# Attention's row sums divided out in the block turning, by a diagonal matrix, instead of on GpSimd

## The chip, the cores and the metric

The kernel runs on one core of a Trainium2 chip. The metric is device time in microseconds for one execution of the whole layer, from runs on the chip. The core's engines are TensorE (PE; its weight loads are listed apart as PEld), VectorE (DVE), ScalarE (ACT), GpSimd (POOL) and SyncE (SP), which here only issues DMAs.

## The reference

One decoder layer: a sequence of 1024 rows of width 1024, in float32. The part that matters is the forgetting attention, 8 heads of width 64:

```
s = einsum('bhqd,bhkd->bhqk', qi, kh) * scale
s = s + ci[..., None] - cum[:, :, None, :]
s = where(key_pos <= q_pos, s, -inf)
p = softmax(s, axis=-1)
out = einsum('bhqk,bhkd->bhqd', p, vh)
```

Beside it stand four retention heads of width 128, computed in chunks of 128 rows; both groups go through one output projection, a layer norm, a gated MLP with a short convolution, and a second layer norm.

## The kernel before, in words

The program is straight-line code. It runs through stages: the conditioning and the retention heads (to about 239 us of the profile), the projection of the attention's values, the attention (about 272 to 492 us), the output projection, the up-projection and the down-projection. Up to the attention, the order of the engines' work is set by hand (a helper that queues each instruction behind the last one) and by a planner; from the attention on, each engine issues its instructions in the order of the program text, except where a line pins one behind another (`tc.issue_after`).

Nearly all large matmuls work on pairs of a high and a low half in the F32R type, so that a product of two F32 values is three matmuls. A few small products of the retention (`pS`, `po`) use plain F32 operands on 128x128 tiles, and so do the transposes, which multiply by the identity `ident` in transpose form (`pq`, `py`, `nT` and the attention's `pt`).

The attention is one loop of 8 heads x 8 row tiles of 128 rows, here called steps, and four more steps to drain it. A step `s_` of head `h` and row tile `i` does this, in the order of the text:

1. a piece of the projection of queries and keys, of this head or the next (`fox_proj`, lines 765 to 767), 6 matmuls of 512 columns;
2. `fox_scores` (lines 796 to 812): the scores of the row tile against the keys up to the diagonal, in a two-bank PSUM tile `ps`; on DVE, the sum with the bias row and the row's minimum `mn` (the scores are negated) into the SBUF tile `S`, 128 x (i+1)*128; on ACT, the exponential of the negated tile, with the row sums `den`; on DVE, the reciprocal of `den`; on GpSimd (line 813), `S` times the reciprocal, in place;
3. at odd steps, `fox_pv` (line 851) of a pair of row tiles: values times probabilities;
4. `fox_turn` (lines 824 to 842) of the row tile of three steps ago (`LAG = 3`): each 128x128 block of `S` is transposed on TensorE into a PSUM bank `pt`, up to four blocks a bank; ACT copies the bank into the high half of the probabilities, and DVE subtracts to make the low half.

There are 36 blocks a head, 288 in all, in 96 banks. `pt` comes from a ring of four PSUM banks, shared with the projections `qk` and the products `pv`. `S` tiles come from rings of SBUF slots; `dn` and `mn` are small tiles of one column.

The only work of GpSimd in this stage is line 813. The retention's small tiles `sT` and `R` (tags `sT` and `Rs`, three buffers each, 128x128 in F32) have their last use before the attention begins.

Of the kernel before, what the change touches and what calls it, by code (L numbers as in the profile page):

```python
# [8 lines left out]
F32 = mybir.dt.float32  # L9
# [4 lines left out]
ALU = mybir.AluOpType  # L14

P = 128
S = 1024
D = 1024
NT = S // P
# [12 lines left out]
def kernel(  # L32
# [23 lines left out]
    nc = tc.nc  # L56
# [5 lines left out]
    sp = ctx.enter_context(tc.tile_pool(name="sp", bufs=1))  # L62
# [4 lines left out]
    def slot(tag, shape, dtype, name, padded=None):  # L67
        return gp.tile(shape, dtype, tag=tag, bufs=NB[tag], name=name, padded_shape=padded)
# [4 lines left out]
    def small(shape, name):  # L73
        return sp.tile(shape, F32, tag="s", bufs=24, name=name)

    def f(ap):
        return ap.bitcast(F32)


    ident = cp.tile([P, P], F32, tag="ident", name="ident")  # L80
# [10 lines left out]
        out=maskb, in_=maskb, pattern=[[-1, P]], compare_op=ALU.is_ge,  # L91
# [5 lines left out]
        out=tri, in_=tri, pattern=[[1, P]], compare_op=ALU.is_ge,  # L97
# [39 lines left out]
    def bank2(name):  # L137
        return ps.tile([P, 1024], F32, tag="A", bufs=2, name=name)

    def bank(name):  # L140
        return ps.tile([P, 512], F32, tag="B", bufs=4, name=name)
# [173 lines left out]
    for i in (0, 2):  # L315
        queued("DVE", nc.vector.tensor_scalar,
               out=bcol[:, i, :], in0=bcol[:, i, :], scalar1=1.0, scalar2=None, op0=ALU.add)
# [24 lines left out]
    for j in range(ND):  # L342
# [28 lines left out]
        for t in range(3):  # L371
            for c in range(7):
                in_turn(first[c], (hi, hi, lo)[t][:, c * P:(c + 1) * P],
                        w0[j][:, (0, 1, 0)[t], :],
                        start=(j == 0 and t == 0), stop=(j == ND - 1 and t == 2))
# [4 lines left out]
    def ret_proj(h, c, ws, part, pt):  # L380
        if part == 0:

            pt = bank(f"rp{h}_{c}") if (h, c) == (0, NT - 1) else bank2(f"rp{h}_{c}")[:, :512]
        for j in range(4 * part, 4 * part + 4):
            three(pt, hhi[j][:, c * P:(c + 1) * P], hlo[j][:, c * P:(c + 1) * P],
                  ws[j][:, 0, :], ws[j][:, 1, :], j == 0, j == ND - 1, in_turn)
        return pt
# [166 lines left out]
    for n in range(RH * NT):  # L554
        h, c = divmod(n, NT)
# [51 lines left out]
    for m in range(NT - 1, RH * NT):  # L607
        h, c = divmod(m, NT)
# [3 lines left out]
        pt = ret_proj(h, c, ws, 0, None)  # L612
# [137 lines left out]
    def fox_alloc(h):  # L750
        t = {n: slot("X", [P, S], F32R, f"{n}{h}") for n in ("qh", "ql", "ks")}
        t["nb"] = slot("X" if h < 2 else "VM", [P, S], F32, f"nb{h}")
        pins["nb"] = nc.sync.dma_start(t["nb"], bass.AP(
            tensor=cum_d.tensor, offset=cum_d.offset + h * S, ap=[[0, P], [1, S]]))
        return t
# [27 lines left out]
    def fox_scores(h, i, T, beside=None):  # L783
        qh, ql, ks, nb = T["qh"], T["ql"], T["ks"], T["nb"]
        span = (i + 1) * P
        tag = "S" if i % 2 == 0 else "R" if h < FH - 1 else "VM"
        Ssb = slot(tag, [P, S], F32, f"S{h}_{i}")
        cuts = [(0, min(max(span, 256), 512))]
        if span > 512:
            cuts.append((512, max(span, 768)))  # L790
        mn = small([P, 1], f"mn{h}_{i}")
        qs = slice(i * P, (i + 1) * P)
        pt = bank2(f"ps{h}_{i}")
        for k0, k1 in cuts:
            last = k0 <= i * P < k1
            nc.tensor.matmul(pt[:, k0:k1], qh[:, qs], ks[:, k0:k1], start=True, stop=False)
            nc.tensor.matmul(pt[:, k0:k1], ql[:, qs], ks[:, k0:k1],
                             start=False, stop=not last)
            if last:
                nc.tensor.matmul(pt[:, i * P:(i + 1) * P], identb, maskb,  # L800
                                 start=False, stop=True)
        pins["min"] = nc.vector.tensor_tensor_reduce(  # L802
            out=Ssb[:, :span], in0=pt[:, :span], in1=nb[:, :span], scale=1.0, scalar=3e38,
            op0=ALU.add, op1=ALU.min, accum_out=mn,
        )
        if beside is not None:
            beside()
        den = small([P, 1], f"dn{h}_{i}")
        pins["exp"] = nc.scalar.activation(  # L809
            Ssb[:, :span], Ssb[:, :span], AF.Exp, scale=-1.0, bias=mn, accum_out=den,  # L810
        )
        nc.vector.reciprocal(den, den)  # L812
        nc.gpsimd.tensor_tensor(  # L813
            out=Ssb[:, :span], in0=Ssb[:, :span], in1=den.to_broadcast([P, span]),
            op=ALU.mult,
        )
        return Ssb

    PT = {}

    def fox_turn(h, i, Ssb):
        g, qo = divmod(i, 2)
        nkb = 2 * g + 2
        if qo == 0:
            PT[h, g] = [[slot("X", [P, 4, 256], F32R, f"pt{h}_{g}_{t}_{u}") for u in range(2)]
                        for t in range((nkb + 3) // 4)]
            for u in range(2):
                nc.vector.memset(  # L828
                    f(PT[h, g][(nkb - 1) // 4][u][:, (nkb - 1) % 4, 0:128]), 0.0)
        for t in range((i + 4) // 4):  # L830
            kbs = range(4 * t, min(4 * t + 4, i + 1))
            n = len(kbs)
            pt = bank(f"pt{h}_{i}_{t}")
            for kb in kbs:
                nc.tensor.transpose(  # L835
                    pt[:, (kb % 4) * P:(kb % 4 + 1) * P], Ssb[:, kb * P:(kb + 1) * P], ident
                )
            src = pt[:, :n * P].rearrange("p (k q) -> p k q", q=P)
            dh = PT[h, g][t][0][:, :n, qo * P:(qo + 1) * P]
            dl = PT[h, g][t][1][:, :n, qo * P:(qo + 1) * P]  # L840
            nc.scalar.copy(dh, src)  # L841
            nc.vector.tensor_tensor(out=dl, in0=src, in1=f(dh), op=ALU.subtract)  # L842

    def fox_pv(h, g):
# [4 lines left out]
        for kb in range(nkb):  # L849
            for u in range(2):  # L850
# [12 lines left out]
                            op=ALU.mult)  # L863
# [124 lines left out]
    def park_high(k):  # L988
        hi, raw = park[k]
        nc.scalar.copy(hi.bitcast(F32R), raw)  # L990

    def park_low(k):

        if k in park:
            hi, raw = park[k]
            with tc.issue_after(pins["min"].ins):
                nc.vector.tensor_tensor(out=raw.bitcast(F32R), in0=raw, in1=hi, op=ALU.subtract)
# [125 lines left out]
    Sb = {}  # L1123

    def proj(h, i):
        if i < 3:
            fox_proj(h, w, T[h], 1, i + 1)
        elif h + 1 < FH:
            fox_proj(h + 1, w, T[h + 1], *divmod(i - 3, 4))

    for s_ in range(FH * NT + LAG + 1):
        h, i = divmod(s_, NT)
        if h < FH:
            if i == 0:
                if h % 4 == 0:
                    for half in range(2):
                        mixF[h // 4, half] = slot("VM", [P, 2, 512], F32, f"mixF{h // 4}_{half}")
            if i == 3:
                w = nw
                if h + 1 < FH:  # L1140
                    T[h + 1] = fox_alloc(h + 1)
            if i >= 3:
                proj(h, i)
            k = LOWS.get(s_)
            Sb[s_] = fox_scores(h, i, T[h], None if k is None else lambda: park_low(k))
            if i == 4 and h + 2 < FH:
                nw = fox_w(h + 2)
            if i == 6:
                down_base(h)
            if k is not None:  # L1150
                park_store(k)
            for v, k in LOWS.items():
                if s_ == max(v - 4, 0):
                    park_load(k)
                if s_ == v - 2:
                    with tc.issue_after(pins["exp"].ins):
                        park_high(k)
        r = s_ - LAG - 1
        if r >= 0 and r % 2 == 1:
            fox_pv(r // NT, (r % NT) // 2)  # L1160
        r = s_ - LAG
        if 0 <= r < FH * NT:
            fox_turn(r // NT, r % NT, Sb.pop(r))
        if h < FH and not (i >= 3):
            proj(h, i)
        if h == FH - 1 and i == 0:
            for q in range(2):
                op_load(q)
            g_row = slot("S", [P, D], F32, "g_row0")
            nc.sync.dma_start(g_row, bcast_rows(gates[0], D))  # L1170
        if h == FH - 1:
            for m in LOADS.get(i, ()):
                wo_load(m)
            if i in (2, 3):
                op_split(i - 2, 1)
            if i >= NT - 2:
                op_half(0, 1, i - NT + 2)
        if s_ == FH * NT:
            for q in range(2):
                x_load(q)  # L1180
                sos[q] = slot("X", [P, S], F32, f"so{q}")
        if s_ == FH * NT + 1:
            op_mm(1, 1)
            op_split(0, 0)
# [440 lines left out]
    for pi, p in enumerate(PORD[:-1]):  # L1625
# [4 lines left out]
        start, stop = p in (1, 2, 5), p in (2, 3)  # L1630
        for k in range(NK):
# [5 lines left out]
            else:  # L1637
                for i in range(4):
                    d_mm(p, k, i, pts[i], start and k == 0, stop and k == NK - 1)
                    if p == 7 and k == NK - 1:  # L1640
                        add = nc.vector.tensor_tensor(  # L1641
                            out=s5[i], in0=s5[i], in1=X_[i], op=ALU.add)
# [105 lines left out]
```

## Time and profile before

| | us |
|---|---|
| median of 3 runs | 1215.36 (1215.21 to 1215.37) |
| span of the profiled execution | 1214.8 |
| runs beyond the span | about 0.6 |
| TensorE busy in the span | 1198.3 |
| DVE busy | 910.9 |
| ACT busy | 653.9 |
| GpSimd busy | 229.0 |
| of that, line 813 | 73.5 |

The profile is of one execution; its span runs from the first to the last instruction, and the device time has a little more around it. Times are in microseconds unless marked ns. A line of a group gives the source line, the engine, the operation, out<-in by the program's names, the shapes, the count, and then either the minimum, median and maximum of its durations, or busy time, mean ns of one and the idle time before it with what ended that. Matmuls overlap in the array, so that their durations are longer than the steps from one to the next. The chain of work that ended last follows the program back from its end, at each step to what released it; there, a row's time is its share of the way to the end, and `issue` is time in which nothing that the profile shows was waited for. The rows of waits give who waited for whom, the total, the times and the longest.

### The profile page before, as it was taken

Reading aid. Unit: us, or ns where it says so; the run is one execution under the profiler, and the core shown is the slowest. Engines: PE = TensorE matmul, PEld = TensorE weight load, DVE = VectorE, ACT = ScalarE, POOL = GpSimd, SP = SyncE. Lnnn points to the kernel's source line nnn. Section 1 sums busy time; section 2 is a strip of 40 time slices with the busy share of each in tenths; the row PEclk is TensorE's granted clock in tenths of the full one; section 3 lists DMA queues with packets and bytes.
Section 4 is the critical chain, followed back from the end, with each engine's and each line's share of the span. In section 5 each row is a group of like instructions: output and inputs, shape, how many; then the busy total and the mean of one; then the engine's idle time right before and its main releaser. Section 6 shows DMA issues by size and latency. Waiting matters only on the chain.

```text
span 1214.8 us, 17196 instructions
## 1 busy us (share of the span) xinstructions
PE 1198.3 (99%) x6005; PEld 1002.4 (83%) x6005; DVE 910.9 (75%) x1757; ACT 653.9 (54%) x1201; POOL 229.0 (19%) x274
## 2 busy tenths in 40 slices
PE   8999999999999999999999999999999999999997
PEld 6888888997888888888888888888888888888875
DVE  7847747766888887456988778787787876886586
ACT  6635444345777766567755545455454565543452
POOL 0015335012333333000021323211000010000021
PEclk9999999999999999999999999999999999999999
DMA  9523444605575658223268887776554489875751
GB/s 358 227 87 122 139 148 143 202 32 175 164 222 164 203 171 335 96 77 115 87 178 204 193 223 185 171 184 175 152 139 128 148 249 297 321 243 178 248 181 69
DMA packets 94279, 216.57 MB, mean 178 GB/s; under 512 B 10784, under 2 KB 17136, under 8 KB 94192
## 3 DMA queue, kind: packets, MB, share of 16 engines
q1 hardware_dynamic: 81520, 192.40, 46.0%
q0 software_dynamic: 12672, 23.07, 11.8%
q8 instruction: 47, 0.77, 0.3%
q14 instruction: 40, 0.33, 0.1%
HBM read 173.45 MB, written 76.59 MB: 206 GB/s over the span
## 4 chain that ended last, share of the span: by engine, by line
PE 87%; DMA 5%; DVE 4%; ACT 1%; issue 1%; SPq 0%; POOL 0%; DVEq 0%; ACTq 0%; POOLq 0%
PE rp L152 11%; PE dX L1489 7%; PE uX L1264 7%; PE uX L1263 7%; PE uX L1265 7%; PE dZ L1489 5%; PE uY L1263 5%; PE uY L1265 5%; PE uY L1264 5%; PE vp L152 4%; PE pv L851 3%; DMA ada<-in_ada_dram 3%; PE pt L835 2%; PE op L189 2%; PE op L191 2%; PE op L190 2%
## 5 line engine op out<-in xcount | busy, mean ns | idle before, releaser
L152 PE MATMUL rp<-wr,hhi 128*128 128x512 f32 x400 | 127.9, 401 | 0.0
L1475 DVE TENSOR_TENSOR dl<-dr,dh 128x1024 fp32r<-128x1024 f32 x66 | 80.3, 1237 | 36.3 <-ACT dh L1463 35.1
L813 POOL TENSOR_TENSOR S<-S,dn 128x128 f32<-128x128 f32 (+3 forms) x64 | 73.5, 1154 | 151.7 <-DVE dn L812 130.1
L1463 ACT CAST dh<-dr 128x1024 fp32r<-128x1024 f32 x58 | 59.6, 1051 | 65.7 <-DMA dr<-td 35.5
L1106 POOL DMA_DIRECT2D sd<-gd x22 | 18.1, 823 | 398.5 <-DMA sd<-y 227.2
L152 PEld LDWEIGHTS rp<-wr,hhi 128*128 128x128 f32 x400 | 71.6, 189 | 12.7
L152 PE MATMUL rp<-wr,hlo 128*128 128x512 f32 x200 | 78.6, 393 | 0.0
L1489 PE MATMUL dX<-dh 128*128 128x512 f32 x176 | 68.5, 389 | 0.8 <-DVE ds L1641 0.8
L1489 PE MATMUL dX<-dl,dh 128*128 128x512 f32 x176 | 68.5, 389 | 0.0
L1489 PE MATMUL dX<-dh,dl 128*128 128x512 f32 x176 | 68.5, 389 | 0.0
L1278 ACT COPY u<-uX 128x512 f32<-128x512 f32 x44 | 25.8, 586 | 70.3 <-PE uX L1265 70.3
L152 DVE CUSTOM_DVE_ANT_0 ada<-ada,csb,bcol 128x1024 f32<-128x1024 f32 x46 | 60.1, 1309 | 3.0 <-DMA ada<-in_ada_dram 3.0
L842 DVE TENSOR_TENSOR pt<-pt,pt 128x512 fp32r<-128x512 f32 (+2 forms) x96 | 50.7, 549 | 10.2 <-ACT pt L841 9.1
L809 ACT ACTIVATE S<-S,mn 128x128 f32<-128x128 f32 (+3 forms) x64 | 49.9, 779 | 11.1 <-DVE mn L802 10.5
L765 PE MATMUL qk<-hhi,wqh 128*128 128x512 f32 x128 | 54.8, 428 | 0.4 <-DVE pt L828 0.4
L767 PE MATMUL qk<-hhi,wql 128*128 128x512 f32 x128 | 51.9, 405 | 0.0
L1489 PE MATMUL dZ<-dh 128*128 128x512 f32 x132 | 51.6, 391 | 0.0
L1489 PE MATMUL dZ<-dl,dh 128*128 128x512 f32 x132 | 51.4, 389 | 0.0
L1489 PE MATMUL dZ<-dh,dl 128*128 128x512 f32 x132 | 51.4, 389 | 0.0
L841 ACT CAST pt<-pt 128x512 fp32r<-128x512 f32 (+2 forms) x96 | 44.1, 478 | 13.4 <-PE pt L835 12.1
L189 PE MATMUL op<-wo,mxs 128*128 128x512 f32 x128 | 51.1, 399 | 0.0
L802 DVE CUSTOM_DVE_ANT_0 S<-ps,nb 128x128 f32<-128x128 f32 (+3 forms) x64 | 47.4, 741 | 4.2 <-PE ps L800 3.5
(1049 smaller groups left out, 3661.7 us busy)
## 6 DMA issues: line engine op xcount, KB each, us to landing
ada<-in_ada_dram SPq DMA_DIRECT2D x48, 512.0 KB, 3.7
td<-in_w_down_dram SPq DMA_DIRECT2D x44, 256.0 KB, 5.4
wa<-in_w_up_dram SPq DMA_DIRECT2D x22, 512.0 KB, 4.7
wb<-in_w_up_dram SPq DMA_DIRECT2D x22, 512.0 KB, 4.1
gd<-y SPq DMA_DIRECT2D x22, 512.0 KB, 3.2
sd<-y SPq DMA_DIRECT2D x44, 256.0 KB, 3.4
dr<-sd SPq DMA_DIRECT2D x44, 256.0 KB, 3.9
dr<-td SPq DMA_DIRECT2D x44, 256.0 KB, 4.3
```

The costliest lines, as they stand in the source:

```text
L152: order[key] = fn(*args, **kw)
L189: mm(pt, ahi, whi, start=start, stop=False)
L765: nc.tensor.matmul(pt, whi[:, j, :], hhi[j][:, sl], start=(j == 0), stop=False)
L767: nc.tensor.matmul(pt, wlo[:, j, :], hhi[j][:, sl], start=False, stop=(j == ND - 1))
L813: nc.gpsimd.tensor_tensor(out=Ssb[:, :span], in0=Ssb[:, :span], in1=den.to_broadcast([P, span]), op=ALU.mult,)
L842: nc.vector.tensor_tensor(out=dl, in0=src, in1=f(dh), op=ALU.subtract)
L1263: nc.tensor.matmul(pt, whi, bh, start=start, stop=False, skip_group_check=True)
L1264: nc.tensor.matmul(pt, whi, bl, start=False, stop=False, skip_group_check=True)
L1265: nc.tensor.matmul(pt, wlo, bh, start=False, stop=stop, skip_group_check=True)
L1463: nc.scalar.copy(hi, raw)
L1475: nc.vector.tensor_tensor(out=lo, in0=raw, in1=f(hi), op=ALU.subtract)
L1489: nc.tensor.matmul(pt, w_[:, 0, q], m_[:, 1, :], start=start and n_ == 0, stop=stop and n_ == 2, skip_group_check=True)
```

## The change

The probabilities are no longer divided on GpSimd in the `S` tile. Instead GpSimd makes a 128x128 tile `dg`, the identity times the reciprocal of the row sums, one a step, in the buffers of the retention's `sT` (even row tiles) or `R` (odd ones). The turning of a block is then a matmul with the undivided block as the stationary operand and `dg` as the moving one: the block's transpose, with column q multiplied by the reciprocal of row q's sum. Block, `dg` and identity are all F32. The number of blocks, the banks and what ACT and DVE do after them stay.

```
@@ fox_scores
         nc.vector.reciprocal(den, den)
-        nc.gpsimd.tensor_tensor(
-            out=Ssb[:, :span], in0=Ssb[:, :span], in1=den.to_broadcast([P, span]),
-            op=ALU.mult,
-        )
-        return Ssb
+        dg = sp.tile([P, P], F32, tag=("sT", "Rs")[i % 2], bufs=3, name=f"dg{h}_{i}")
+        nc.gpsimd.tensor_tensor(out=dg, in0=ident, in1=den.to_broadcast([P, P]), op=ALU.mult)
+        return Ssb, dg
...
-    def fox_turn(h, i, Ssb):
+    def fox_turn(h, i, Ssb, dg):
...
             for kb in kbs:
-                nc.tensor.transpose(
-                    pt[:, (kb % 4) * P:(kb % 4 + 1) * P], Ssb[:, kb * P:(kb + 1) * P], ident
+                nc.tensor.matmul(
+                    pt[:, (kb % 4) * P:(kb % 4 + 1) * P], Ssb[:, kb * P:(kb + 1) * P], dg,
+                    start=True, stop=True,
                 )
...
-            fox_turn(r // NT, r % NT, Sb.pop(r))
+            fox_turn(r // NT, r % NT, *Sb.pop(r))
```

## The prediction

> **What bounds the kernel now.** I read the page from the top: the busy shares, the slices, then the chain of work that ended last.
>
> ```profile
> span 1214.8 us, 17196 instructions
> PE 1198.3 (99%) x6005; PEld 1002.4 (83%) x6005; DVE 910.9 (75%) x1757; ACT 653.9 (54%) x1201; POOL 229.0 (19%) x274
> ...
> PEclk9999999999999999999999999999999999999999
> ...
> PE 87%; DMA 5%; DVE 4%; ACT 1%; issue 1%; SPq 0%; POOL 0%; DVEq 0%; ACTq 0%; POOLq 0%
> ```
>
> TensorE is busy nearly all the time at the full granted clock, and it holds 87% of the chain; GpSimd holds 0%. A busy TensorE alone proves little, because its matmuls are pipelined, so I went to the attention stage itself: first the busy times of 272 to 492 us, then the chain there.
>
> ```profile
> 272.00:492.00 220.00, 218.31 (x1307) 182.84 (x1306) 174.12 (x480) 151.18 (x342) 73.51 (x64) 1.00 0.61 201
> ```
>
> The columns are PE, PEld (its weight loads), DVE, ACT and POOL busy, then clock, DMA share and GB/s. DVE works 174 of 220 us, ACT 151, and GpSimd's 64 row products 73.5. The chain inside one whole head, 376 to 402 us, decides who is last:
>
> ```profile
> by line: PE pv L851 19.5%; PE pt L835 18.4%; PE qk L765 14.8%; PE qk L767 14.3%; PE qk L766 14.2%; PE ps L796 8.4%; PE ps L797 8.4%; PE ps L800 2.2%
> ```
>
> Every entry is TensorE, and the shares add to 100. The block turning (L835) is 18% of it. So in this stage a TensorE instruction more is time more, and a GpSimd microsecond less is worth only what some other engine waited for it.
>
> **The second pass.** The change replaces each transpose (F32 block against the identity) by an ordinary F32 matmul with the block stationary and the diagonal moving, also F32. How many instructions each of the two is, can be counted in the retention stage, which has both kinds on 128x128 tiles.
>
> ```profile
> L152 PE MATMUL pq<-ident,rst x64: 270/272/273, 56.0 to 229.1; 128*128 128x128 f32 x64
> L428 ACT COPY qkT<-pq x32: 351/374/406, 56.6 to 229.4; 128x256 f32<-128x256 f32 x32
> ...
> L152 PE MATMUL pS<-qkT x64: 270/275/275, 58.9 to 232.6; 128*128 128x128 f32 x64
> L152 DVE TENSOR_TENSOR sT<-pS,dec x32: 256/258/293, 62.8 to 233.1; 128x128 f32<-128x128 f32 x32
> ```
>
> Two transposes fill each 256-wide pq that ACT copies 32 times, and there are 64 records: one record a transpose. One F32 matmul fills each 128-wide pS that DVE reads 32 times, and there are again 64: two records, that is two passes, each with its own weight load. The duration of one (272, 275 ns) is latency, not price; the price is the step from one to the next in the chain.
>
> ```profile
> 151.05 0.44 PE po L152 x4
> 151.49 0.45 PE pS L152 x4
> 151.94 0.44 PE py L152 x4
> ...
> 346.79 0.44 PE pt L835 x4
> ```
>
> The po and pS rows are four F32 matmuls (8 passes) in 0.89 us, 0.2225 each. The py row and the pt row are four transposes in 0.44 us, 0.110 each. A block turned by matmul therefore costs 0.1125 us more. The blocks are 8 heads x (1+2+...+8) = 288:
>
> ```profile
> L835 PEld LDWEIGHTS pt<-ident,S x288: 137/140/144, 286.7 to 488.3; 128*128 128x128 f32 x144
> L835 PE MATMUL pt<-ident,S x288: 270/272/331, 286.8 to 488.4; 128*128 128x128 f32 x144
> L835 PEldq EVENT_SEMAPHORE  x58: 51/51/51, 290.9 to 485.4; - x58
> ```
>
> 288 x 0.1125 = +32.4 us on the bounding engine, with no cover: the other engines' work lies under TensorE, not over it.
>
> The Trainium skill (Perfetto Trace Analysis, section Transposes) says a logical transpose should be issued as a transpose and not as a standard matmul, because it skips the arithmetic; the rows agree, with a factor of two. The Trainium skill (FP8 and Floating Point Precision, section TensorE Precision Notes) gives true FP32 four passes; by that the term would be 288 x 3 x 0.110 = 95 us, by the rows it is 32.4, and the measurement decides, here with two passes.
>
> **The GpSimd product goes, a smaller one comes.** By width the rows of L813 are eight each; the narrowest and the widest:
>
> ```profile
> L813 POOL TENSOR_TENSOR S<-S,dn 128x1024 f32<-128x1024 f32 x8 | 15.3, 1909 | 16.0 <-DVE dn L812 10.0 <-PE ps L800 6.0
> ...
> L813 POOL TENSOR_TENSOR S<-S,dn 128x128 f32<-128x128 f32 x8 | 3.2, 400 | 28.2 <-DVE dn L812 28.2
> ```
>
> The new product is 128x128 in every step: 64 x 0.400 = 25.6 us in place of 73.5, so GpSimd saves 48 us. It is the only GpSimd work of the stage, and it waits for its inputs, not the others for it. Of all lines only one waited for it, DVE's weight split, for 0.5 us; the chain passes through it once:
>
> ```profile
> 290.50 1.04 POOL S L813
> ...
> 291.58 1.26 POOL S L813
> 292.85 0.24 issue
> 293.09 0.10 DVE wql L644
> ...
>   DVE wql L644: 0.5, 1
> ```
>
> The gain lies between 0 and the 2.3 us of those two chain pieces; I count it in the next term. The transpose of a row runs three steps of some 3.2 us (26 us for eight) after its scores, so it did not wait for the product and does not gain from an earlier one.
>
> **Stalls that a longer TensorE covers.** Where TensorE waits for DVE or ACT in this stage, 4 us more of TensorE work a head gives these engines time to catch up.
>
> ```profile
> PE pt L835 <- DVE ks L777: 1.0, 2, 0.6
> PE qk L765 <- DVE pt L828: 0.4, 1, 0.4
> ...
> PEld pt L835 <- issue: 2.2, 5, 0.8
> PEld pt L835 <- DVE pt L842: 1.9, 6, 0.4
> PEld pv L851 <- DVE pt L842: 1.4, 5, 0.4
> PEld qk L765 <- ACT qh L771: 0.6, 1, 0.6
> PEld ps L796 <- issue: 0.5, 1, 0.5
> PEld op L189 <- DVE mixF L858: 0.3, 1, 0.3
> PEld ps L797 <- DVE ql L781: 0.2, 1, 0.2
> PEld pt L835 <- DVE mixF L858: 0.2, 1, 0.2
> ```
>
> These add to 8.7 us, the most that can go. What goes in fact I take from the length of a head, between the same 16 products in the chain:
>
> ```profile
> 362.64 1.97 PE pv L851 x16
> 388.84 1.97 PE pv L851 x16
> 414.40 1.97 PE pv L851 x16
> 440.55 1.97 PE pv L851 x16
> ```
>
> The heads take 26.20, 25.56 and 26.15 us; the middle one is nearly without stalls, so the mean excess is 0.41 us, 3.3 us for eight. Some of them come from DVE being late at the head's change and will stay in part: I take -2.5 us, between 0 and -8.7.
>
> **New waits.** The first turn of a group must now see two producers, ACT's exponential and GpSimd's diagonal, where it saw GpSimd alone. A second semaphore shows as one more 51 ns entry on TensorE's sequencer; 58 exist already. Behind it would stand the rest of TensorE's order, the next projection and scores, and so every engine. For all 96 groups that is 96 x 0.051 = 4.9 us at most. I take 0, since with 58 of them the chain by engine above lists no TensorE sequencer at all; at the other end a gain is excluded, because nothing is taken out. A diagonal that is late is the other possible wait: it comes after the row's maximum, exponential and reciprocal, as the product did, and is shorter by 0.75 us in the mean, with nothing else queued on GpSimd.
>
> **Edits at nothing.** The diagonal lives in the six buffers of the retention's sT and R tiles, idle by now; one is used again after six steps and freed after three. The PSUM bank of a group is held 0.45 us longer; the four rotating banks also turn more slowly, and the 1.9 us of waits on them are in the stall rows; were they to double, that is +1.9, inside the range. Reciprocal, exponential, the high and low halves (L841, L842) and all DMA stay: no transfer and no queue of SP is moved, and DVE's count is equal. After the stage TensorE is the bound again, so nothing is given back there.
>
> **The sum.** Span 1214.8, and 0.6 around it to the median of the runs shown, 1215.36. 1214.8 + 0.6 + 32.4 - 2.5 + 0 = 1245.3 us. The ends: 1215.4 + 32.4 - 8.7 = 1239 and 1215.4 + 32.4 + 4.9 = 1253.
>
> **Rivals.**
> First, not slower: the second pass hides. If the two passes of one block stepped no slower than one transpose, the term is 0, and with the stalls and the product gone the time is 1215.4 - 2.5 = 1213 (0.2% is some 2.4 us, about what a measurement of this kernel can tell from no change). For it speaks that a narrow matmul can step faster than 0.11:
>
> ```profile
> 343.60 0.07 PE ps L800
> ```
>
> That is a bf16 block of 128 columns. Against it stand the po and pS rows, F32 as here, at 0.11 a pass. It decides below 2.5/288 = 0.009 us more a block. Chance 3 in 100.
>
> Second, the stage was held by GpSimd after all, and the product's 48 us return in part. The 0% in the chain and the one 0.5 us waiter speak against it; it would need over 30 us of hidden waits to offset the passes, where all TensorE waits are 8.7. With all these gone it ends at 1239, still slower; 5 in 100 for its being the larger part.
>
> Third, a new wait takes the lead: TensorE waits for the diagonal or a bank in most of the 64 rows, say 0.3 us each, +19 us, 1245 + 19 = 1264. GpSimd's idle time speaks against it. 4 in 100.
>
> Fourth, four passes a block: 3 x 0.110 x 288 = 95 more, less 2.5, 1308 us. Only the Trainium skill's page named above has this; the count of two for each retention product excludes it unless these instructions are formed otherwise. 2 in 100.
>
> The forecast as summed keeps 86 in 100. The range 1239 to 1253 leaves out rivals one, three and four and a little of the spread. Slower 0.96, within 0.2% 0.02, faster 0.02.
>
> **What would show it.** Right: the turn's group counts 576 matmuls and 576 weight loads, a load nearer 190 ns than 140; four blocks in the chain take 0.89 us where they took 0.44; the stage grows from 220 to about 250 us and all others keep their length; GpSimd's busy time falls from 229 to about 181. Wrong: 288 records (rival one), 1152 (rival four), or waits of TensorE for the diagonal (rival three). A stage whose TensorE waits stay near 8.7 us would make the stall term wrong and the time 1248.

## The result, and the profile after

| | before | changed |
|---|---|---|
| median, us | 1215.36 (1215.21 to 1215.78, 4 runs) | 1245.47 (1244.73 to 1246.13, 4 runs) |
| ratio to before | | 1.0243, 95% interval 1.0231 to 1.0255 |
| span of the profiled execution | 1214.8 | 1243.2 |

The changed kernel is 2.4% slower, 30.1 us. The forecast was 1245.3, between 1239 and 1253. The spans differ by 28.4 us; the other 1.7 lie outside the span. That the sum came out so near is partly luck: the cover of stalls was taken too small, an effect of the issue order was missing, the time around the span was too low, and these nearly cancelled.

The page of the changed kernel: busy shares, the chain by engine, and three groups (line, engine, operation, busy time and mean ns of one, idle time before it).

```profile
PE 1229.9 (99%) x6293; PEld 1037.2 (83%) x6293; DVE 914.0 (74%) x1757; ACT 656.6 (53%) x1201; POOL 181.1 (15%) x274
...
PE 94%; DVE 2%; DMA 2%; ACT 1%; issue 0%; POOL 0%; DVEq 0%; SPq 0%; POOLq 0%
...
L833 PE MATMUL pt<-dg,S 128*128 128x128 f32 x576 | 80.1, 278 | 0.0
...
L833 PEld LDWEIGHTS pt<-dg,S 128*128 128x128 f32 x576 | 72.1, 192 | 2.8 <-issue 1.7
...
L814 POOL TENSOR_TENSOR dg<-ident,dn 128x128 f32<-128x128 f32 x64 | 25.6, 400 | 224.7 <-DVE dn L812 193.8
```

The turning has 576 matmuls and 576 weight loads where it had 288 of each, a load takes 192 ns where it took 140, and GpSimd is busy 181 us where it was 229. TensorE's share of the chain rose from 87 to 94%. The stage is read from the chain. In the changed kernel the same 16 products (`pv`) come at these times; the last row is the last head's:

```profile
344.22 1.97 PE pv L850 x16
373.73 1.97 PE pv L850 x16
403.22 1.97 PE pv L850 x16
432.73 1.97 PE pv L850 x16
...
518.93 1.99 PE pv L850 x16
```

The heads in the middle take 29.5 us, and each the same; before, those that the prediction lists took 25.56 to 26.20. The last product ends at 520.92 us. Before, the same product stood here in the chain, and ended at 491.95:

```profile
489.79 2.16 PE pv L851 x16
```

So 29.0 us were added up to the end of the attention, and from there to the end of the span it is 722.3 us against 722.9: next to nothing came or went in the later stages.

TensorE's waits of 272 to 523 us, in the changed kernel:

```profile
PEld L800 <- issue: 6.8, 32, 0.3
PEld pt L833 <- issue: 1.7, 5, 0.4
PEld ps L796 <- issue: 0.5, 1, 0.5
PEld pv L850 <- DVE pt L841: 0.5, 2, 0.2
PEld pt L833 <- PE qk L767: 0.4, 1, 0.4
PEld pt L833 <- DVE pt L841: 0.2, 1, 0.2
```

The first row belongs to the small load of the mask's matmul. It stood at 6.2 before, behind `issue`, and is left out, since the chain of the heads has no idle time of TensorE at it. Without it, the waits that were 8.7 us are 3.3.

### The profile page after: what moved, and what is told of

The parts are those of the page before. It is cut to its first block, busy times and chain, and to the rows that moved or that the text cites. A ratio compares the mean times of both kernels' runs of the same rounds, so it can differ in the third digit from the quotient of the medians.

```text
span 1243.2 us, 17825 instructions
## 1 busy us (share of the span) xinstructions
PE 1229.9 (99%) x6293; PEld 1037.2 (83%) x6293; DVE 914.0 (74%) x1757; ACT 656.6 (53%) x1201; POOL 181.1 (15%) x274
## 4 chain that ended last, share of the span: by engine, by line
PE 94%; DVE 2%; DMA 2%; ACT 1%; issue 0%; POOL 0%; DVEq 0%; SPq 0%; POOLq 0%
PE rp L152 11%; PE dX L1488 10%; PE dZ L1488 7%; PE uX L1263 6%; PE uX L1262 6%; PE uX L1264 6%; PE pt L833 5%; PE uY L1262 5%; PE uY L1264 5%; PE uY L1263 5%; PE vp L152 4%; PE pv L850 3%; PE qk L765 2%; PE qk L767 2%; PE qk L766 2%; PE op L189 2%
## 5 line engine op out<-in xcount | busy, mean ns | idle before, releaser
L1474 DVE TENSOR_TENSOR dl<-dr,dh 128x1024 fp32r<-128x1024 f32 x66 | 80.6, 1239 | 35.7 <-ACT dh L1462 33.8
L833 PE MATMUL pt<-dg,S 128*128 128x128 f32 x576 | 80.1, 278 | 0.0
L833 PEld LDWEIGHTS pt<-dg,S 128*128 128x128 f32 x576 | 72.1, 192 | 2.8 <-issue 1.7
L814 POOL TENSOR_TENSOR dg<-ident,dn 128x128 f32<-128x128 f32 x64 | 25.6, 400 | 224.7 <-DVE dn L812 193.8
```

Of the source, the lines that this page charges most:

```text
L833: nc.tensor.matmul(pt[:, (kb % 4) * P:(kb % 4 + 1) * P], Ssb[:, kb * P:(kb + 1) * P], dg, start=True, stop=True,)
L1474: nc.vector.tensor_tensor(out=lo, in0=raw, in1=f(hi), op=ALU.subtract)
```

## The experiments

The theory at this point: the second F32 pass is the price, some of it covered by stalls. The rivals: waits for the diagonal or the plain matmul itself (A), the type of the operands (B), and a hidden worth of GpSimd's load (C).

**One pass a block (e1_one_pass).** Scores, probabilities and diagonal in F32R.

```
-            out=Ssb[:, :span], in0=pt[:, :span], in1=nb[:, :span], ...
+            out=Ssb[:, :span].bitcast(F32R), in0=pt[:, :span], in1=nb[:, :span], ...
-            Ssb[:, :span], Ssb[:, :span], AF.Exp, ...
+            Ssb[:, :span].bitcast(F32R), Ssb[:, :span], AF.Exp, ...
-        dg = sp.tile([P, P], F32, ...
+        dg = sp.tile([P, P], F32R, ...
-                    ..., Ssb[:, kb * P:(kb + 1) * P], dg,
+                    ..., Ssb[:, kb * P:(kb + 1) * P].bitcast(F32R), dg,
```

> The changed kernel with both operands of the block turning in the F32R type: DVE's sum with the bias row, ACT's exponential and the diagonal are written as F32R, so scores and probabilities are rounded to that type's shorter mantissa; everything else stays, the wait for the diagonal too. Theory (the second F32 pass is the price): 288 turning matmuls instead of 576, each stepping like the transposes at about 0.11 us, so the 32 us go and the covered GpSimd product stays out: 1211 to 1215 us. Rival A (an ordinary matmul with a freshly made diagonal costs time through its waits, not its passes): 1235 us or more. Rival B (a pass of an ordinary matmul costs twice a transpose's step whatever its type): about 1245 us.

Measured: 1227.22 us (1226.88 to 1227.97), ratio to before 1.0093, interval 1.0079 to 1.0107. This is none of the three. The passes are one a block (288 records), rival B is out, yet 11 us remain. TensorE waits more than in the kernel before. Without L800 its rows add to 25.9 us, against 8.7; a matmul and its weight load that wait for the same thing are both counted, so this is more than the loss in time. The longest in 272 to 510 us:

```profile
PE pv L851 <- DVE pt L842: 4.2, 8, 0.7
PE pt L834 <- DVE pt L842: 3.2, 7, 0.6
...
PEld pt L834 <- issue: 6.5, 12, 0.8
PEld pv L851 <- DVE pt L842: 6.1, 9, 0.9
```

Products and turns wait for DVE's low halves. No row names GpSimd, so none is a wait for the diagonal that the profile shows; the `issue` row it does not explain, and f2 below has it too, without a diagonal.

**Second passes without the diagonal (e2_matmul_ident).**

```
-                nc.tensor.transpose(
-                    pt[...], Ssb[:, kb * P:(kb + 1) * P], ident
-                )
+                nc.tensor.matmul(
+                    pt[...], Ssb[:, kb * P:(kb + 1) * P], ident,
+                    start=True, stop=True,
+                )
```

> The kernel before, with its GpSimd product over the row tile, and only the transposes replaced by plain F32 matmuls of the block against the identity: the changed kernel's passes without its diagonal and without its relief of GpSimd. Theory: the same 576 matmuls on the bounding engine, so the changed kernel's time, 1245.5 us within 2. Rival A (waits for the diagonal make part of the rise): below 1240. Rival C (the smaller GpSimd product gave something back): above the changed kernel by that amount, 1248 to 1255.

Measured: 1246.23 us (1245.97 to 1248.02), ratio 1.0252, interval 1.0238 to 1.0266. The rise is all there without a diagonal and with GpSimd's full product. Rival A is out, and rival C is out as a part that the times could show. The trace shows a little more: with the changed kernel's order and waits, the heads in the middle take 29.65 us where the changed kernel's take 29.50, and its last product ends 0.9 us later (521.80 against 520.92), which fits a small part of C.

```profile
374.02 1.97 PE pv L852 x16
403.65 1.97 PE pv L852 x16
```

**No product (e3_no_product).** Line 813 left out, so nothing is divided; transposes as before.

```
-        nc.gpsimd.tensor_tensor(
-            out=Ssb[:, :span], in0=Ssb[:, :span], in1=den.to_broadcast([P, span]),
-            op=ALU.mult,
-        )
```

> The kernel before without the GpSimd product at all: the probabilities are not divided by their row sums, nothing else changes and the blocks are transposed as before. It bounds what the removal of the product can be worth. Theory: between 0 and the 2.3 us that the chain spent in it: 1213 to 1215.4 us. Rival C (GpSimd's load holds something): 1210 us or less.

Measured: 1213.90 us (1213.43 to 1215.03) beside 1216.12 for the kernel before on the same chip; ratio 0.9983, interval 0.9974 to 0.9992. All 73.5 us of GpSimd's work are worth 2.2 us. Little of this comes from the two pieces of the chain in GpSimd, at 290 to 293 us, that gave the bound. The times of the same product as in the prediction:

```profile
362.01 1.97 PE pv L847 x16
387.66 1.97 PE pv L847 x16
413.11 1.97 PE pv L847 x16
438.75 1.97 PE pv L847 x16
```

Up to the first of these, 0.6 us are gained (362.64 before). Then the two long heads, 26.20 and 26.15 us, fall to 25.65 and 25.64, half a microsecond each, and the short one from 25.56 to 25.45. TensorE's waits in the stage, without L800, fall from 8.7 to 5.6 us.

**Each block turned twice (e4_twice).**

```
+                for _ in range(2):
                     nc.tensor.matmul(..., dg, start=True, stop=True)
```

> The changed kernel with each turning matmul issued twice into the same place, the second result overwriting the equal first: 1152 turning passes. Theory (a pass is worth its step of 0.111 us once no stall is left to cover): 1245.5 + 288 x 0.2225 = 1309.6 us within 2. If longer fills of the PSUM banks brought waits of their own, more than 1314; if the price of a pass fell with more of them in a row, less than 1305.

Measured: 1308.96 us (1308.22 to 1309.62), ratio 1.0764, interval 1.0749 to 1.0779. That is 63.5 us above the changed kernel for 576 more passes, 0.110 us each, against 0.111 foreseen. With few stalls left to cover (3.3 us in the changed kernel), a pass costs about its step. The longest run of turns in its chain, eight blocks of four passes, gives 0.113 a pass:

```profile
391.14 3.63 PE pt L834 x32
```

**What e1 left open: the issue order.** The section on the kernel before says that from the attention on the engines issue in the order of the text. That is wrong: the planner interleaves there too. The kernel before, in TensorE's timeline, puts seven products and a turn between the second and the third matmul of a projection piece:

```profile
350.80 0.40 PE L766 MATMUL qk<-hlo,wqh 128*128 128x512 f32 x1
351.04 0.99 PE L851 MATMUL pv<-pt,V 128*128 128x256 f32 x7
351.87 0.28 PE L835 MATMUL pt<-ident,S 128*128 128x128 f32 x1
351.90 0.47 PE L767 MATMUL qk<-hhi,wql 128*128 128x512 f32 x1
```

Comparing the programs instruction by instruction, there are two orders. The kernels with transposes (before and e3) have one, called A here; those with a plain matmul of one issue a block (changed, e1, e2) have another, B, the same on all engines. e2 has no diagonal and still B: the plain matmul moved the order. e4, with two issues a block, has a third, so its 63.5 us hold a change of order besides the passes; against the changed kernel in order A (f3 below) it is 66.0 us, 0.115 a pass. In B turns are put between the products, as in the changed kernel:

```profile
351.01 0.36 PE L850 MATMUL pv<-pt,V 128*128 128x256 f32 x1
351.21 0.39 PE L833 MATMUL pt<-dg,S 128*128 128x128 f32 x2
351.35 0.60 PE L850 MATMUL pv<-pt,V 128*128 128x256 f32 x3
351.79 0.61 PE L833 MATMUL pt<-dg,S 128*128 128x128 f32 x4
```

The new theory is that e1's 11 us are B's. Three kernels cross the two orders with the three ways to turn. Each is an earlier kernel with one addition behind the attention's loop: edges of issue order alone (no wait for an end) along the list of the other order, on TensorE, DVE, ACT and SP.

```
+    for eng_, ranks_ in ORDER.items():
+        mine_ = [i for i in traced_ if str(i.engine) == "EngineType." + eng_]
+        for a_, b_ in zip(ranks_, ranks_[1:]):
+            tc.add_manual_dep(mine_[b_], mine_[a_].name,
+                mybir.DependencyInfo(mybir.DependencyClass.NoSync, ...), ...)
```

**One pass in order A (f1_one_pass_orderA).**

> The kernel with one F32R pass a block and the diagonal, with the issue order of the kernel before pinned on TensorE, DVE, ACT and SP through the attention (order A); without the pin it has, instruction for instruction, the issue order of the changed kernel (order B). New theory: the 11 us by which it was slower than the kernel before are order B's, which sets turns and products ahead of DVE's halves; with order A it is 1212 to 1216 us. Rival (a matmul with the diagonal waits or costs more than a transpose): about 1227 us again.

Measured: 1216.25 us (1214.80 to 1217.66) beside 1216.15 for the kernel before; ratio 1.0000, interval 0.9992 to 1.0009. A plain matmul with the diagonal, at one pass, costs what a transpose with the full product costs. The 2.2 us that e3 gained do not appear here. Whether the diagonal, the F32R matmul or GpSimd's smaller product uses them up, no run tells apart.

**The kernel before in order B (f2_before_orderB).**

> The kernel before, transposes and GpSimd product as they were, with the changed kernel's issue order (order B) pinned on the same four engines. New theory: order B alone costs what the one-pass kernel lost: 1223 to 1229 us. Rival (order does not matter; the diagonal or the plain matmul does): 1215 to 1218 us.

Measured: 1226.60 us (1226.37 to 1226.87), ratio 1.0081, interval 1.0067 to 1.0095. Order B alone costs 10.4 us, and the waits are e1's: the largest of TensorE's load side in its 272 to 520 us (the early load that costs nothing is left out):

```profile
PEld pv L987 <- DVE pt L978: 8.5, 16, 0.9
...
PEld pt L971 <- issue: 6.8, 12, 0.9
```

In its timeline a product waits 0.66 us for DVE's low half, and a turn 0.47:

```profile
353.57 1.10 PE L987 MATMUL pv<-pt,V 128*128 128x256 f32 x7 [0.66 <-DVE pt L978]
...
357.70 0.41 PE L971 MATMUL pt<-ident,S 128*128 128x128 f32 x2 [0.47 <-DVE pt L978]
```

**The changed kernel in order A (f3_after_orderA).**

> The changed kernel with the issue order of the kernel before (order A). If the second pass alone makes the rise and 4 us more of TensorE work a head cover either order's waits: 1244 to 1248 us, as with order B. If order B had brought a loss that is still in the changed kernel: 1235 to 1241. If order B had saved something: 1250 or more.

Measured: 1242.96 us (1242.56 to 1243.11), ratio 1.0215, interval 1.0201 to 1.0229, below the 1244 to 1248 foreseen and above the 1235 to 1241 of the other case. Its waits in the stage, two heads of the chain, and its last product:

```profile
PEld L936 <- issue: 6.3, 29, 0.3
PEld ps L932 <- issue: 0.5, 1, 0.5
PEld pt L969 <- issue: 0.3, 1, 0.3
PEld pv L986 <- DVE pt L977: 0.2, 1, 0.2
...
402.10 1.97 PE pv L986 x16
431.37 1.97 PE pv L986 x16
...
516.82 1.99 PE pv L986 x16
```

The waits are 1.0 us where B leaves 3.3, and the attention ends at 518.81, 2.1 us before the changed kernel's. So the doubled passes cover nearly all of order A's stalls and most, not all, of order B's. Side by side, as times over the kernel before that ran beside each:

| | order A | order B |
|---|---|---|
| transposes | 0 | +10.4 |
| one F32R pass with the diagonal | +0.1 | +11.1 |
| two F32 passes with the diagonal | +26.8 | +30.1 (the change) |

Read down, the second pass adds 27 us in order A and 19 in order B (30.1 less 11.1; e2, on e1's chip, gives the same 19.0): in the order that waits more, a pass costs less. The change is the step from the upper left to the lower right. Its cell comes from the first comparison, where the kernel before was 0.8 us faster than beside the f runs. Read across, the lowest row therefore overstates the order: 3.3 us by these times, but 1.9 by the spans (1243.2 against 1241.3) and 2.1 by the end of the last product. About 2 us is the better figure.

## Why the prediction was right, by its steps

- **The bound.** Right. The added TensorE work came through to the end of the span, and 73.5 us of GpSimd came through with 2.2 us when taken away whole (e3). That is within the 0 to 2.3 that the chain's two pieces gave, but by luck: the gain came mostly in the long heads, and little of it at these pieces.
- **Two passes a block, 0.1125 us more.** Right. The count is 576, and e4 prices a pass at 0.110 to 0.115 in the same stage. The Trainium skill (FP8 and Floating Point Precision, section TensorE Precision Notes) has four passes for true FP32; the trace has two records a block, and the 95 us of that reading did not come. The retention's products, counted beforehand, had decided it.
- **The stalls covered, -2.5.** Mis-sized, and for a reason that the step did not see. In the order in which the waits were read, the cover is larger: 32.4 - 26.8 = 5.6 us, of the 8.7 that were the end of the range. It holds what the smaller GpSimd product gave, as the forecast's term did. The head-length reading (3.3 us, cut to 2.5) was too careful: it took the head of 25.56 us, with a chain of TensorE alone, for one nearly without stalls, while f3's heads of 29.27 us, less 36 second passes (4.05 us), are 25.22.
- **New waits, 0.** Right for what was named: no wait of TensorE for the diagonal shows (e2 has the rise without one, f1 equals the kernel before), and the sequencer's entries at the turns rise from 58 to 59 in order A (f1 and f3), not by one a group. What did come was not named: the change of order, +10.4 by itself, of which about 2 us are left under two passes. The edits were read as local to two functions; the planner made them an edit of the whole stage's order. By what it orders instructions was not looked into.
- **Around the span, 0.6.** Too low. It was 2.3 for the changed kernel (1245.47 less 1243.2). In the 30 runs of the kernel before beside the experiments, each listed with its own span, it is 1.7 as well, so most of it is not the change's. The 0.6 set the span of one profiled execution beside the median of the runs; for the kernel before, the first comparison does not list both for each run.

With sizes as measured, the span is 1214.8 + 32.4 - 5.6 + 2 = 1243.6, where the profile has 1243.2, and 2.3 around it give 1245.9. The mechanism that the forecast named, the second pass, gives nearly all of the rise. The near hit of 1245.3 is luck as to the last 3 us: a cover that was 3.1 us too small stood against an order effect of about 2 that was missing and 1.7 too little around the span.

The rivals: the hidden second pass is out by e4 and the counts, GpSimd as the bound by e3, waits for the diagonal by e2 and f1, four passes by the count of records.

## What to carry to other kernels

Before a transpose becomes a matmul, count the instructions that the product takes in its operand type: in F32 it was two passes with two weight loads here, and on a full TensorE each costs its step (0.11 us for 128 columns), while work taken from an idle engine pays nearly nothing. Read an added instruction against the waits of its own stage, since it first fills those. And where a planner sets the issue order, compare the orders of the two programs before explaining a difference: replacing one kind of instruction moved the order of four engines, which was worth 10 us under transposes and about 2 of the change's 30.

## What the runs showed of the hardware

A 128-column pass with four-byte operands steps at about 0.11 us whether it is a transpose, an F32R matmul or one of the two F32 passes (f1's chain has seven F32R passes in 0.73 us, the kernel before four transposes in 0.44; e4 gives 0.110 to 0.115), although the weight load's own record grows from 140 ns for the transpose to 192 ns for the others. The longer load record does not show in the step.
